# Front-projected DeltaNet columns stay raw until the mixers convolve them; decay matrices are made in other blocks, their rows loaded by SyncE

## The chip, the cores and the metric

The kernel runs on one NeuronCore of a Trainium2 chip. The metric is the device time of one execution in microseconds. Five engines run side by side, each from its own in-order queue: TensorE (PE, matmuls), VectorE (DVE), ScalarE (ACT), GpSimd (POOL) and SyncE (SP, which only starts transfers). They wait for each other through semaphores. A transfer can be started from the queue of SP, ACT or POOL.

## The reference

One decoder layer on 512 tokens of width 2048, all in float32. Cut to what matters here:

```
u    = rmsnorm(x, norm_w)
proj = u @ w_in                      # 2048 x 20528: q/k/v/o/z of 8 mLSTM heads,
                                     # q/k/v/z of 16 DeltaNet heads, gates, merge gates
# mLSTM branch: chunkwise, with exp(b_t - b_s + i_s) as decay matrix per head
# DeltaNet branch, 16 heads of 128:
qkv  = silu(causal_conv4(dn_qkv, dn_conv_w))       # 4 taps along the tokens, per channel
q, k = l2norm(q), l2norm(k)
gam  = cumsum(g)                                   # g <= 0, per head
D[t,s] = exp(gam[t] - gam[s]) for s <= t, else 0   # decay matrix per head
A    = strict_lower(beta * (k k^T) * D);  solve (I + A) w = rhs;  then chunk by chunk
h_b  = rmsnorm(o, dn_norm_w) * silu(dn_z)
out  = rmsnorm(x + sigmoid(ga) * (h_a @ w_out[:2048]) + sigmoid(gb) * (h_b @ w_out[2048:]))
```

## The kernel before

**Precision and bounds of the work.** Each float32 operand of a large matmul is split into a high and a low part (`split_hi` at L147 on ACT, `split_lo` at L150 on DVE), and each product is three matmuls (high by high, low by high, high by low). The activations are split once (`uh`, `ul`); the weights come in as raw tiles by SP and are split just ahead of their use.

**Stages, in PE's order.**
1. The front: seven projections of 256 DeltaNet columns each straight from the activations (`FRONT`, L170): the pair of k columns of heads 0 and 1, and v columns of six odd heads with those of other heads beside them, eight columns of 128 in all that are needed later (`PRE`). `spill` (L391) writes them raw, scaled by the token factor, to `raw_d` in DRAM.
2. The first stage: 14 blocks of `SEVEN`, each a Strassen-like 1024 x 1024 piece of the projection (`seven`, L617). A block has an A half of 8 quads with four products each, and a B half of 8 quads with three. A product is six 128 x 512 matmuls (L643 to L645), and after each one `tick()` lets the side tasks go on by one step. So a block has 56 ticks, 336 matmuls, and its A half ends at tick 32. The blocks are, in order: four for mLSTM z and o ("z"), two for DeltaNet z ("s"), one for mLSTM q and k ("q"), two for v, one "q", four for the merge gates ("g"). I call them blocks 0 to 13.
3. The mixers: eight units (`dn_unit`, L1304), unit p holding the DeltaNet heads 2p and 2p+1. In each, PE projects k, v and q columns while side tasks run the convolution, norms, triangular solve and recurrence of the heads; eight `ml_head` tasks run beside them.
4. The output projection: three plain blocks, two of the Strassen kind and a last one.

**The crossing.** In a block the PSUM results of the A half must be added up before the B half goes on in the same banks. ACT copies two of them (`copy1`, L628), and DVE does three pairs of additions through `add` (L700): m1 into `U1`, then U1 + m5 into `C22`, then m7 onto `C22`. B's matmuls on m5 wait for the second pair, those on m7 for the third. I call this place the crossing.

**Side tasks.** A task is a generator; its `yield n` asks to be resumed n ticks later, and `start` puts it on the list. PE's order is written by hand. On the other engines a scheduler orders the instructions by priority and its own estimate of when they are ready; `urgent` and `high_priority` raise some, and `behind("V")` (or "A", "S") makes an instruction come after the newest weight split of DVE (cast of ACT, weight load of SP). Weight splits and `add` have a raised priority. The table `ahead` (L940) says which side task starts in which block, at quad 5 of its A half (tick 20), but in the last block at its first quad:

- blocks 0 to 4: five `decay(n)` each (four in the last), one after the other. A decay matrix is made in a 128 x 512 tile: POOL loads the row of `gam` to all partitions (L885), 3 ticks later POOL masks it (`affine_select`, L892), 2 ticks later ACT takes the exponentials, all in one step (four activations at L902, or for odd DeltaNet heads, which are mirrored, twelve at L898 to L900), and ACT's queue stores it to `dm_d`.
- blocks 5 to 12: `scaled_u(2i)` and then `convolved(i)`. `scaled_u` (L853) makes the scaled activations of two of the sixteen 128-rows for a later stage: per row DVE adds (L863), multiplies (L866) and subtracts (L871), ACT casts (L868), two stores. `convolved` (L907) loads one raw column tile from `raw_d`, does the four taps (one ACT multiplication at L915, three DVE instructions at L918), silu on ACT (L922) and a 32 x 32 block transposition on DVE (L925), and stores the transposed tile to `pre_d` in 4 transfers with pieces of 128 bytes from ACT's queue (and, for the k columns, the plain tile to `kc_d`).
- block 13: `scaled_back`, which reads the scaled activations into `uh` and `ul`.

Those tasks and the block ends (`sink_...`) share four tiles of 128 x 512 (tag "wr", `spare` at L703).

**A unit of the mixers.** `conv_in` (L1010) copies a projected column tile from PSUM into one of two padded tiles `yp`; `conv_silu` (L1017) does the taps (ACT L1021, three DVE instructions L1023); `silu_end` (L1026) does silu (ACT L1028) and calls `turn` (L1041), which transposes 32 x 32 blocks on DVE (L1044) and sends the tile through DRAM, 4 writes of 128-byte pieces (L1060) and a read (L1063), all from SP. `dn_front_k` (L1066) forms k k^T (PE L1086), scales it, writes the diagonal blocks to DRAM and solves them on DVE in 31 steps of two small instructions (L1135, L1137); the result goes through DRAM (`xd`, L1149, and `tt`, L1150, from SP) and is transposed on DVE into `tn` (L1153). `dn_back` (L1178) starts with matmuls on `tn` (PE L1191). For the eight columns made ahead, `turned` (L1299) loads the finished tile from `pre_d`; unit 0 takes k from `kc_d`, and for units 1 to 6 (`VPRE`) the v columns of the odd head are the ones made ahead, so their v projection has one head only (`proj_half`).

## Time and profile before

| | us |
|---|---|
| median of 3 runs | 2180.43 |
| lowest, highest | 2177.93, 2183.38 |
| the profiled execution's own time | 2176.61 |
| its span, first to last instruction | 2174.4 |
| PE busy in it | 2124.8 (98%) |
| DVE busy | 1747.1 (80%) |
| ACT busy | 1102.4 (51%) |
| POOL busy | 503.1 (23%) |
| blocks 0 to 13 of the first stage | 116 to 1226 |
| mixers | 1226 to about 1860 |

How to read it: PE has work nearly all the time, and its instructions are fixed, so the time moves only where PE waits or where its clock is lowered. The waits of PE, and what ended each, are therefore read first, then PE's busy time in short stretches around the places where it waits, then what the engine that it waited for did there. The other engines' busy shares matter only where PE waits for them. In the block table of the page a PE share of 9 means 90% or more and hides waits of 2 us, so stretches of one block (76 to 81 us) or less are used. Starts of the A halves of blocks 0 to 13 are at 116, 200, 278, 358, 436, 512, 591, 670, 749, 830, 909, 988, 1068 and 1147 us, and of the B halves at 167, 247, 325, 405, 481, 558, 637, 715, 794, 875, 953, 1033, 1114 and 1192 us, read from the first matmuls on `su` and `s4` tiles.

### The profile page before, as it was taken

How to read it: one execution, taken by the hardware profiler on the slowest of the kernel's cores; microseconds unless marked ns; L12 is line 12 of the kernel's file. 1: busy time of each engine (PE TensorE's matmuls, PEld its weight loads, DVE VectorE, ACT ScalarE, POOL GpSimd, SP SyncE). 2: the span in 40 equal slices, each digit the busy share in tenths (PEclk: the TensorE clock that was granted, in tenths of full speed). 3: DMA queues.
4: the chain of work that ended last, by engine and by line, in shares of the span. 5: the costliest groups of instructions: out<-in, count | busy, mean ns of one | idle time of the engine just before them, and what ended most of it. 6: DMA issues, size and time to landing. Idle time of an engine off the chain costs nothing.

```text
span 2174.4 us, 32578 instructions
## 1 busy us (share of the span) xinstructions
PE 2124.8 (98%) x10507; PEld 1748.0 (80%) x10507; DVE 1747.1 (80%) x3022; ACT 1102.4 (51%) x2135; POOL 503.1 (23%) x745
## 2 busy tenths in 40 slices
PE   9999999999999999999999999999999999999998
PEld 7777778888778778787778888887888888887786
DVE  5978888798898888888788586796787789569787
ACT  4445665655554545444444444543644555345345
POOL 1231121010004000220000123434434444233221
PEclk9999999999999999999999999999999999999999
DMA  5466776777778867787769877877777868778796
GB/s 175 146 200 214 241 237 222 248 234 230 235 249 245 272 210 238 234 256 240 248 212 329 301 191 180 204 176 198 210 199 204 206 166 233 203 216 288 229 294 237
DMA packets 473828, 491.74 MB, mean 226 GB/s; under 512 B 192485, under 2 KB 304842, under 8 KB 473530
## 3 DMA queue, kind: packets, MB, share of 16 engines
q1 hardware_dynamic: 375898, 357.67, 55.5%
q0 software_dynamic: 28416, 83.65, 12.3%
q10 hardware_dynamic: 69344, 48.36, 6.9%
q8 instruction: 82, 1.34, 0.3%
q14 instruction: 88, 0.72, 0.1%
HBM read 376.71 MB, written 117.02 MB: 227 GB/s over the span
## 4 chain that ended last, share of the span: by engine, by line
PE 47%; DVE 4%; DMA 3%; issue 1%; ACT 1%; SPq 0%; DVEq 0%; POOLq 0%; POOL 0%; ACTq 0%
PE pj L292 11%; PE pj L290 6%; PE ps L644 5%; PE ps L643 5%; PE ps L645 5%; PE py L1580 2%; PE py L1582 2%; PE py L1581 2%; DMA wr<-in_w_out_dram 2%; PE pj L274 1%; PE pj L273 1%; PE pj L272 1%; DVE wl L150 1%; PE pk L1086 1%; PE pqk L1161 1%
## 5 line engine op out<-in xcount | busy, mean ns | idle before, releaser
L147 ACT CAST wh<-wr 128x512 fp32r<-128x512 f32 (+1 forms) x506 | 368.2, 729 | 374.4 <-PE pj L292 157.0
L150 DVE TENSOR_TENSOR wl<-wr,wh 128x512 fp32r<-128x512 f32 (+1 forms) x506 | 426.5, 844 | 157.3 <-ACT wh L147 145.2
L643 PE MATMUL ps<-wh,uh 128*128 128x512 f32 x800 | 314.4, 393 | 18.6 <-DVE X L700 18.6
L644 PE MATMUL ps<-wl,uh 128*128 128x512 f32 x800 | 313.5, 392 | 3.3 <-DVE wl L150 3.2
L645 PE MATMUL ps<-wh,ul 128*128 128x512 f32 x800 | 312.9, 391 | 0.0
L290 PE MATMUL pj<-uh,wh 128*128 128x512 f32 x672 | 284.7, 424 | 1.3 <-ACT qk L406 1.3
L147 ACT CAST wh<-t 128x1024 fp32r<-128x1024 f32 x128 | 135.0, 1055 | 293.9 <-PE ps L645 114.2
L292 PE MATMUL pj<-uh,wl 128*128 128x512 f32 x672 | 264.8, 394 | 0.6 <-DVE wl L150 0.6
L644 PE MATMUL ps<-wl,suh 128*128 128x512 f32 x672 | 262.2, 390 | 1.9 <-DVE wl L150 1.8
L292 PE MATMUL pj<-ul,wh 128*128 128x512 f32 x672 | 264.1, 393 | 0.0
L643 PE MATMUL ps<-wh,suh 128*128 128x512 f32 x672 | 262.0, 390 | 2.1 <-ACT wh L147 2.1
L645 PE MATMUL ps<-wh,sul 128*128 128x512 f32 x672 | 261.8, 390 | 0.0
L147 ACT CAST wh<-ts 128x512 fp32r<-128x512 f32 x256 | 158.2, 618 | 163.9 <-DVE ts L603 129.4
L598 POOL DMA_DIRECT2D t_d<-ts x112 | 61.7, 551 | 736.7 <-DVE ts L585 671.4
L150 DVE TENSOR_TENSOR wl<-t,wh 128x1024 fp32r<-128x1024 f32 x128 | 158.2, 1236 | 75.4 <-ACT wh L147 75.2
L150 DVE TENSOR_TENSOR wl<-ts,wh 128x512 fp32r<-128x512 f32 x256 | 176.1, 689 | 37.1 <-ACT wh L147 35.2
L643 PEld LDWEIGHTS ps<-wh,uh 128*128 128x128 f32 x800 | 150.7, 188 | 56.5 <-DVE X L700 25.1
L644 PEld LDWEIGHTS ps<-wl,uh 128*128 128x128 f32 x800 | 151.0, 189 | 36.5 <-DVE wl L150 5.7
L645 PEld LDWEIGHTS ps<-wh,ul 128*128 128x128 f32 x800 | 151.0, 189 | 31.5
L584 DVE TENSOR_TENSOR t<-wr 128x1024 f32<-128x1024 f32 x128 | 157.0, 1227 | 15.7 <-DMA wr<-in_w_in_dram 8.7
L644 PEld LDWEIGHTS ps<-wl,suh 128*128 128x128 f32 x672 | 126.2, 188 | 29.9 <-DVE wl L150 3.9
L643 PEld LDWEIGHTS ps<-wh,suh 128*128 128x128 f32 x672 | 126.1, 188 | 29.7 <-ACT wh L147 3.4
(372 smaller groups left out, 4141.6 us busy)
## 6 DMA issues: line engine op xcount, KB each, us to landing
wr<-in_w_in_dram SPq DMA_DIRECT2D x728, 256.0 KB, 4.0
wr<-in_w_out_dram SPq DMA_DIRECT2D x138, 256.0 KB, 5.0
t_d<-ts POOLq DMA_DIRECT2D x112, 256.0 KB, 4.3
wr<-t_d SPq DMA_DIRECT2D x112, 256.0 KB, 4.4
wr<-in_w_in_dram SPq DMA_DIRECT2D x48, 128.0 KB, 2.3
to<-rows_d POOLq DMA_DIRECT2D x24, 256.0 KB, 5.3
dm_d<-to ACTq DMA_DIRECT2D x24, 256.0 KB, 3.2
us_d<-uhi ACTq DMA_DIRECT2D x16, 256.0 KB, 3.6
```

Of the source, the lines that this page charges most:

```text
L147: newest["A"] = A.copy(hi, src).ins
L150: newest["V"] = V.tensor_tensor(out=lo, in0=src, in1=hi.bitcast(F32), op=ALU.subtract).ins
L290: T.matmul(ps[j], hi[:, k, wsl], uh[:, kt, :], start=(kt == 0), stop=False)
L292: T.matmul(ps[j], w[:, k, wsl], x_[:, kt, :], start=False, stop=(kt == KT - 1 and w is lo))
L584: V.tensor_tensor(out=t13, in0=r[:, 1:3, :], in1=r[:, 0:2, :], op=ALU.subtract)
L598: queue.dma_start(t2_d[b % 2, i], ts[:, 0, :])
L643: T.matmul(ps[t], ah, hi, start=(g == "A" and i == 0), stop=False, skip_group_check=True)
L644: T.matmul(ps[t], ah, lo, start=False, stop=False, skip_group_check=True)
L645: T.matmul(ps[t], al, hi, start=False, stop=(i == KH - 1), skip_group_check=True)
L1580: T.matmul(ps[c], uh[:, kt, tsl], hi, start=(kt == ks[0]), stop=False)
L1581: T.matmul(ps[c], uh[:, kt, tsl], lo, start=False, stop=False)
L1582: T.matmul(ps[c], ul[:, kt, tsl], hi, start=False, stop=(kt == ks[-1]))
```

## The change

- `convolved` is gone, with `pre_d` and `kc_d`. The eight column tiles stay raw in `raw_d`. In the mixers `conv_loaded` (new) loads one from `raw_d` into a `yp` tile by SP, 4 ticks later does the taps, 4 or 6 ticks later silu and `turn`, which is what the unit's own columns go through. For units 1 to 6 it starts 2 ticks after the k projection, ahead of the v projection; `dn_front_k` of unit 0 starts 6 ticks later than before, and its `dn_back` 5 ticks later.
- `scaled_u` moves from blocks 5 to 12 to blocks 1 to 8 and starts at quad 7 of the A half (tick 28) where it was quad 5.
- `decay` moves from blocks 0 to 4 to blocks 0, 9, 10, 11 and 12. The row is loaded by SP behind the newest weight load, not by POOL; the mask comes 5 ticks after it, not 3. The exponentials of the four chunks are 1 tick apart each, not in one step. The five decays of a block are started 6 ticks apart, so that they can overlap. The positive column for mirrored heads is copied once by DVE in `gates`, not made by POOL for each head.

```
-        G.dma_start(flat, rows_d[row, :].partition_broadcast(P))
-        if mirror:
-            pgam = sbp.tile([P, NC], F32, tag="pgam", name="pgam", bufs=1)
-            G.tensor_scalar(out=pgam, in0=bias, scalar1=-1.0, scalar2=None, op0=ALU.mult)
-        yield 3
+        with behind("S"):
+            nc.sync.dma_start(flat, rows_d[row, :].partition_broadcast(P))
+        yield 5
...
-        with behind("A"):
-            for c in range(NC):
+        for c in range(NC):
+            with behind("A"):
                 if mirror:
...
+            if c < NC - 1:
+                yield 1
+        with behind("A"):
             nc.scalar.dma_start(dm_d[n], flat)
         yield 1
-    def convolved(i):
...
-    ND = 5
-    ahead = [in_turn([decay(n) for n in range(ND * b, min(ND * b + ND, DNH + MLH))]) for b in range(ND)]
-    ahead += [in_turn([scaled_u(2 * i), convolved(i)]) for i in range(KH)]
-    ahead += [None] * (len(SEVEN) - len(ahead))
+    def decays(b):
+        for n in range(ND * b, min(ND * b + ND, DNH + MLH)):
+            start(decay(n))
+            yield 6
+
+    SLOTS = [0, *range(KH + 1, len(SEVEN) - 1)]
+    ND = -(-(DNH + MLH) // len(SLOTS))
+    ahead = [None] + [scaled_u(k) for k in range(0, KT, 2)] + [None] * (len(SEVEN) - KH - 1)
+
+    for i, b in enumerate(SLOTS):
+        ahead[b] = decays(i)
...
-                if b < len(beside) and beside[b] and n == (KH - 3 if b + 1 < len(beside) else 0):
+                if b < len(beside) and beside[b] and n == (0 if b + 1 == len(beside) else KH - 1 if 0 < b <= KH else KH - 3):
...
-    def turned(dst, i):
+    def conv_loaded(i, ct, dst, to, more=0):
+        yp = yps[cnt["yp"] % NYP]
+        cnt["yp"] += 1
         with behind("S"):
-            nc.sync.dma_start(dst, pre_d[i].rearrange("(n j) r a c -> (j r) n (a c)", n=NC))
-        yield 1
+            nc.sync.dma_start(yp[:, 3:S + 3], raw_d[i])
+        yield 4
+        conv_silu(None, ct, dst, yp=yp)
+        yield 4 + 2 * more
+        yield from silu_end(dst, (to if i > 1 else dst, to))
...
-                nc.sync.dma_start(kq[j][:, 0, :], kc_d[j])
-                start(turned(ke, j), 3 + j, front)
-        start(dn_front_k(hs, kq, u), 1, front)
+                start(conv_loaded(j, 16 + hs[j], kq[j][:, 0, :], ke, j), 1 + j, front)
+        start(dn_front_k(hs, kq, u), 1 if p else 7, front)
+        if p in VPRE:
+            vt = u["pool"].tile([P, NC, P], F32, tag="vn", name="vt", bufs=2)
+            start(conv_loaded(VPRE[p], 32 + hs[1], vt.rearrange("p c t -> p (c t)"), vt), 2, front)
+            u["vs"].append(vt)
...
-        start(dn_back(hs, kq, u), 28 - (p == 0) + last, by)
+        start(dn_back(hs, kq, u), 28 + 4 * (p == 0) + last, by)
```

PE's instructions stand in the same order up to the first matmul of unit 0's k k^T; after it, those of unit 0's tasks come some ticks later between the same projections, and over the last third of the program the order is the same again. The scheduled engines are reordered. In rows of the change the line numbers are those of the changed file: the weight split L150 is L148 there, L603 is L604, `add` L700 is L701, L863 is L864, L1149 and L1150 are L1124 and L1125, L1060 and L1063 are L1035 and L1038.

DVE at the crossing of block 5 (the additions are `X<-X,ps`, the chores of `scaled_u` write `ulo`), before:

```order
L150 TENSOR_TENSOR wl<-wr_5141,wh 128x1024
L603 TENSOR_TENSOR ts<-wr_5188 128x512
L863 TENSOR_TENSOR ulo<-uh,ul 128x512
L871 TENSOR_TENSOR ulo<-ulo,uhi 128x512
L700 TENSOR_TENSOR X<-X,ps 128x512 x2
L866 TENSOR_TENSOR ulo<-ulo,rr_5151 128x512
L150 TENSOR_TENSOR wl<-ts,wh 128x512
L700 TENSOR_TENSOR X<-X,ps 128x512 x2
L150 TENSOR_TENSOR wl<-wr_5188,wh 128x1024
L603 TENSOR_TENSOR ts<-wr_5233 128x512
L871 TENSOR_TENSOR ulo<-ulo,uhi 128x512
L700 TENSOR_TENSOR X<-X,ps 128x512 x2
```

and the same place in the change:

```order
L148 TENSOR_TENSOR wl<-wr_4941,wh 128x1024
L604 TENSOR_TENSOR ts<-wr_4986 128x512
L701 TENSOR_TENSOR X<-X,ps 128x512 x3
L148 TENSOR_TENSOR wl<-ts,wh 128x512
L701 TENSOR_TENSOR X<-X,ps 128x512 x3
L148 TENSOR_TENSOR wl<-wr_4986,wh 128x1024
L604 TENSOR_TENSOR ts<-wr_5024 128x512
L864 TENSOR_TENSOR ulo<-uh,ul 128x512
```

The first chore now stands behind all six additions, and so do the wide weight split and the subtraction for the quad after it. Before, blocks 5, 6, 8, 9, 11 and 12 had the order shown first, blocks 7 and 10 one much like it, blocks 0 and 2 a wide split and a subtraction ahead of the last addition but no chore, and blocks 1, 3, 4 and 13 the order shown second. In the change all blocks have the second order but blocks 9 and 11, which have that of blocks 0 and 2.

SP in the third unit of the mixers, between the k projection and the read of the solved blocks (`tt`), before:

```order
L1060 DMA td<-ke 32x16x32 x4
L195 DMA wr<-in_w_in_dram 128x2x256
L1149 DMA xd<-xi 256x1x32 x2
L1063 DMA ke<-td 128x4x128
L1149 DMA xd<-xi 256x1x32
L195 DMA wr<-in_w_in_dram 128x2x256
L1060 DMA td<-ke 32x16x32 x4
L1149 DMA xd<-xi 256x1x32
L1301 DMA vt<-pre_d 128x4x128
L1063 DMA ke<-td 128x4x128
L195 DMA wr<-in_w_in_dram 128x2x256
L1150 DMA tt<-xd 128x8x32
```

and in the change, from the new load of the raw tile on:

```order
L1278 DMA yp_11062<-raw_d 128x512
L193 DMA wr<-in_w_in_dram 128x2x256
L1035 DMA td<-ke 32x16x32 x4
L193 DMA wr<-in_w_in_dram 128x2x256
L1038 DMA ke<-td 128x4x128
L193 DMA wr<-in_w_in_dram 128x2x256
L1124 DMA xd<-xi 256x1x32
L1035 DMA td<-ke 32x16x32 x4
L1124 DMA xd<-xi 256x1x32 x2
L1038 DMA ke<-td 128x4x128
L193 DMA wr<-in_w_in_dram 128x2x256
L1124 DMA xd<-xi 256x1x32
```

The load of the raw tile stands ahead of the k tiles' trip, where the load of the finished tile stood behind it, and one of the four `xd` writes stands ahead of the second trip where two had. The `tt` read follows two loads of `g_d` later, and behind it come eight `td` writes for two v tiles where four stood before.

More of the change, by code (lines that the diff above doesn't have):

```diff
@@ L96, in hybrid_body @@
     raw_d = dr.tile([len(PRE), P, S], F32, tag="rawd", name="raw_d")
-    pre_d = dr.tile([len(PRE), 16, BS, 4, BS], F32, tag="pred", name="pre_d")
-    kc_d = dr.tile([2, P, S], F32, tag="kcd", name="kc_d")
     ident = cp.tile([P, P], F32, tag="ident", name="ident")
@@ L453, in hybrid_body @@
     beta = cp.tile([P, NC, DNH], F32, tag="beta", name="beta")
+    pgam = sbp.tile([P, NC, DNH], F32, tag="pgam", name="pgam")
     def gates():
@@ L539, in gates @@
         A.activation(negeg, pc[:, :, 16:32], AF.Exp)
+        V.tensor_copy(pgam, pc[:, :, 16:32])
         V.tensor_scalar(out=ngam, in0=pc[:, :, 16:32], scalar1=-1.0, scalar2=None, op0=ALU.mult)
@@ L899, in decay @@
                     A.activation(t[64:P, c, 64:P], t[64:P, c, 64:P], AF.Exp, bias=bias[64:P, c:c + 1])
-                    A.activation(t[64:P, c, 0:64], t[64:P, c, 0:64], AF.Exp, scale=-1.0, bias=pgam[64:P, c:c + 1])
+                    A.activation(t[64:P, c, 0:64], t[64:P, c, 0:64], AF.Exp, scale=-1.0, bias=pgam[64:P, c, n:n + 1])
                 else:
                     A.activation(t[:, c, :], t[:, c, :], AF.Exp, bias=bias[:, c:c + 1])
+            if c < NC - 1:
+                yield 1
@@ L903, in decay @@
+        with behind("A"):
             nc.scalar.dma_start(dm_d[n], flat)
         yield 1
-    def convolved(i):
-        raw = wp.tile([P, S], F32, tag="wr", name="pr0", bufs=NRAW)
-        with behind("S"):
-            nc.sync.dma_start(raw, raw_d[i])
-        yield 4
-        ct = PRE[i]
-        y = wp.tile([P, S], F32, tag="wr", name="py0", bufs=NRAW)
-        with behind("A"):
-            A.mul(y, raw, convc[:, 144 + ct:145 + ct])
-        for j in (2, 1, 0):
-            with behind("V"):
-                V.scalar_tensor_tensor(out=y[:, 3 - j:S], in0=raw[:, 0:S - 3 + j], scalar=convc[:, 48 * j + ct:48 * j + ct + 1],
-                                       in1=y[:, 3 - j:S], op0=ALU.mult, op1=ALU.add)
-            yield 1
-        with behind("A"):
-            A.activation(y, y, AF.Silu)
-        yield 1
-        with behind("V"):
-            V.transpose(raw, y)
-        if i < 2:
-            with behind("A"):
-                nc.scalar.dma_start(kc_d[i], y)
-        yield 2
-        ov = raw.rearrange("p (m c) -> p m c", c=BS)
-        for a in range(4):
-            with behind("A"):
-                nc.scalar.dma_start(pre_d[i, :, :, a, :].rearrange("m r c -> r m c"), ov[a * BS:(a + 1) * BS])
-            yield 1
@@ L936, in in_turn @@
-    def in_turn(jobs):
-        for job in jobs:
-            yield from job
-    ND = 5
-    ahead = [in_turn([decay(n) for n in range(ND * b, min(ND * b + ND, DNH + MLH))]) for b in range(ND)]
-    ahead += [in_turn([scaled_u(2 * i), convolved(i)]) for i in range(KH)]
-    ahead += [None] * (len(SEVEN) - len(ahead))
+    def decays(b):
[3 more added lines that the diff above has]
+    SLOTS = [0, *range(KH + 1, len(SEVEN) - 1)]
@@ L1318, in dn_unit @@
             else:
-                nc.sync.dma_start(kq[j][:, 0, :], kc_d[j])
-                start(turned(ke, j), 3 + j, front)
-        start(dn_front_k(hs, kq, u), 1, front)
+                start(conv_loaded(j, 16 + hs[j], kq[j][:, 0, :], ke, j), 1 + j, front)
[4 more added lines that the diff above has]
+            u["vs"].append(vt)
         ps = proj_half(DN_V + dcol) if p in VPRE else proj_cm(DN_V + dcol, evens=p == UNITS[0])
-        for j in range(2):
+        for j in range(len(ps)):
             vt = u["pool"].tile([P, NC, P], F32, tag="vn", name="vt", bufs=2)
-            u["vs"].append(vt)
-            if j < len(ps):
-                conv_silu(ps[j], 32 + hs[j], vt.rearrange("p c t -> p (c t)"))
-                start(silu_end(vt.rearrange("p c t -> p (c t)"), (vt, vt)), 4 + 3 * j, front)
-            else:
-                start(turned(vt, VPRE[p]), 6, front)
+            u["vs"].insert(j, vt)
+            conv_silu(ps[j], 32 + hs[j], vt.rearrange("p c t -> p (c t)"))
+            start(silu_end(vt.rearrange("p c t -> p (c t)"), (vt, vt)), 4 + 3 * j, front)
         if last:
```

1 line of the change is left out of this document (removed).

## The prediction

> **What bounds the kernel now.** First the head of the page, then the view of what PE waited for (columns: total us, times, longest us).
>
> ```profile
> span 2174.4 us, 32578 instructions
> ...
> PE ps L643 <- DVE X L700: 21.2, 20, 1.9
> PE ps L644 <- DVE wl L150: 5.7, 8, 1.6
> PE p L1191 <- DVE tn L1153: 2.9, 1, 2.9
> ...
> PE ps L643 <- ACT wh L147: 2.1, 3, 1.0
> ```
>
> PE waits little, and most of it for the additions of the crossing; the other rows are tens of times shorter. The program's PE order hardly moves, so I price stretches of the first stage by their length. The view of busy time in chosen stretches (columns: stretch, length, then busy us and instructions of PE, weight loads, DVE, ACT and POOL, granted clock, DMA share, GB/s) gives blocks 1, 2, 3, block 4, and blocks 5 to 12 together:
>
> ```profile
> 200.00:278.00 78.00, 76.78 (x338) 63.01 (x337) 63.95 (x81) 50.47 (x98) 15.78 (x24) 1.00 0.72 232
> 278.00:358.00 80.00, 77.72 (x336) 62.07 (x335) 66.19 (x84) 50.66 (x91) 14.69 (x22) 1.00 0.74 231
> 358.00:436.00 78.00, 76.87 (x338) 63.09 (x337) 65.61 (x83) 46.78 (x84) 12.00 (x19) 1.00 0.73 241
> 436.00:512.00 76.00, 76.00 (x337) 62.92 (x336) 65.00 (x83) 43.13 (x72) 9.77 (x16) 1.00 0.73 235
> 512.00:1147.00 635.00, 617.16 (x2689) 505.36 (x2688) 541.55 (x705) 316.35 (x451) 76.46 (x128) 0.99 0.76 239
> ```
>
> Block 4 has PE busy for all of its 76.0 us, so 76 us is a block without a wait. Blocks 1 to 3 together are 236 − 3 × 76 = 8.0 us longer, blocks 5 to 12 are 635 − 8 × 76 = 27.0 us longer. That is the stock from which the change can gain.
>
> The same view around crossings: of block 4, of block 5, then the sum of eight such 12 us stretches (blocks 5 to 12), and the sum of two (blocks 0 and 2).
>
> ```profile
> 477.00:489.00 12.00, 12.00 (x55) 9.93 (x54) 10.63 (x16) 6.57 (x12) 0.00 (x0) 1.00 0.75 238
> ```
>
> ```profile
> 554.00:566.00 12.00, 9.71 (x42) 7.41 (x41) 10.79 (x17) 4.33 (x7) 0.00 (x0) 1.00 0.87 264
> ```
>
> ```profile
> sum 96.00, PE 79.72 PEld 61.10 DVE 93.56 ACT 38.53 POOL 0.00; mean PE 9.97 PEld 7.64 DVE 11.70 ACT 4.82 POOL 0.00
> ```
>
> ```profile
> sum 24.00, PE 19.66 PEld 13.69 DVE 18.27 ACT 15.37 POOL 1.75; mean PE 9.83 PEld 6.85 DVE 9.13 ACT 7.69 POOL 0.88
> ```
>
> In blocks 5 to 12 DVE is busy for 93.56 of 96 us while PE stands for 16.3 of them (96 − 79.72). In blocks 0 and 2 PE stands for 4.3 us of 24, 2.2 each, with DVE busy for only three quarters. So there are two kinds of late addition: one behind too much DVE work, one behind work that itself waits. The timeline of DVE at block 5's crossing (start, us, operation) shows the first kind:
>
> ```profile
> 553.95 0.69 DVE L871 TENSOR_TENSOR ulo<-ulo,uhi 128x512 fp32r<-128x512 f32 x1
> 554.55 1.28 DVE L700 TENSOR_TENSOR X<-X,ps 128x512 f32<-128x512 f32 x2
> 555.75 0.69 DVE L866 TENSOR_TENSOR ulo<-ulo,rr 128x512 f32<-128x512 f32 x1
> ...
> 556.95 1.28 DVE L700 TENSOR_TENSOR X<-X,ps 128x512 f32<-128x512 f32 x2
> 558.14 1.22 DVE L150 TENSOR_TENSOR wl<-wr,wh 128x1024 fp32r<-128x1024 f32 x1
> 559.28 0.68 DVE L603 TENSOR_TENSOR ts<-wr 128x512 f32<-128x512 f32 x1
> 559.88 0.69 DVE L871 TENSOR_TENSOR ulo<-ulo,uhi 128x512 fp32r<-128x512 f32 x1
> 560.48 1.28 DVE L700 TENSOR_TENSOR X<-X,ps 128x512 f32<-128x512 f32 x2
> ```
>
> The last pair, for which B's matmuls on m7 wait, starts 5.9 us after the first (560.48 − 554.55), behind two chores of `scaled_u` (L866 and the second L871), a wide split and a subtraction. In block 4 the second three additions start 2.4 us after the first three:
>
> ```profile
> 477.19 1.88 DVE L700 TENSOR_TENSOR X<-X,ps 128x512 f32<-128x512 f32 x3
> ...
> 479.58 1.87 DVE L700 TENSOR_TENSOR X<-X,ps 128x512 f32<-128x512 f32 x3
> ```
>
> **The crossings.** In the change the order of every block but 9 and 11 is the one that block 4 has, with the chores behind the additions. I therefore take the whole excess of blocks 5 to 12 away, −27.0, and give back two crossings of the kind of blocks 0 and 2 for blocks 9 and 11. Such a crossing costs its 2.2 us of idle and some refilling: the eight crossings' 16.3 us of idle belong to 27.0 − 3.4 (the clock, below) = 23.6 us of excess, though part of that is waits elsewhere in the block, so I take 2.7 each, +5.4. Block 0's crossing loses its lateness too, −2.7. Bounds: the order decides nothing, 0; no crossing late, −29.7.
>
> **The clock inside these 27 us.** Twice among blocks 5 to 12 the granted clock fell right after a crossing; a third time in the mixers:
>
> ```profile
> 795.00:805.00 10.00, 8.12 (x28) 6.20 (x28) 6.45 (x10) 3.36 (x5) 0.00 (x0) 0.83 0.73 240
> 1034.00:1044.00 10.00, 8.12 (x29) 6.18 (x28) 6.45 (x10) 3.44 (x5) 0.00 (x0) 0.83 0.72 237
> 1468.00:1482.00 14.00, 11.14 (x112) 8.65 (x110) 6.98 (x24) 6.34 (x20) 8.13 (x11) 0.76 0.79 186
> ```
>
> 0.17 of 10 us is 1.7 us each, 3.4 us for the first two. PE's idle in those stretches is under 2 us (10 − 8.12), and the longest wait for X is 1.9 us, so the fall followed a short wait here; without the wait I expect no fall. *A rule against this:* the Trainium skill, page "TensorE: Matmul & The Clock Gate", section "HAM oscillation — how this bites in real kernels", gives idle gaps over about 3.4 us as what lowers the clock. By it the falls would not be due to these waits; the rows show shorter ones ahead of each, so the measurement goes against the figure. I keep "the falls stay" as a rival, priced from the rows.
>
> **Blocks 1 to 3.** Block 2 loses a crossing like block 0's. Blocks 1 and 3 have no late crossing; what they wait for is a lump of twelve exponentials of a mirrored decay in ACT's queue ahead of a cast (first, last, and the cast behind them):
>
> ```profile
> 234.30 0.40 ACT L898 ACTIVATE to<-to,ngam 64x128 f32<-64x128 f32 x1
> ...
> 238.01 0.33 ACT L900 ACTIVATE to<-to,pgam 64x64 f32<-64x64 f32 x1
> 238.36 0.62 ACT L147 CAST wh<-ts 128x512 fp32r<-128x512 f32 x1
> ```
>
> 4.1 us of ACT stand ahead of that cast. The decays leave these blocks, so I take all 8.0 us away. Bounds: 0 to −8.0.
>
> **What the moved tasks cost where they go.** `scaled_u` brings six DVE and two ACT instructions to the B half of blocks 1 to 8: 6 × 0.69 = 4.1 us of DVE (the rows of L866 and L871), over some ten ticks of 76 / 56 = 1.36 us. The B quads are three ticks, 4.1 us, long, and carry a wide split, a subtraction and a narrow split: 1.22 + 0.68 + 0.69 = 2.6 us. Each quad thus has 1.5 us of DVE free, and 4.1 us fit into three of them. Nothing but a chance collision is left: 0.25 us a block, +2. If that cover were gone, 4.1 us a block. The decays in blocks 9 to 12 bring ACT the same exponentials in four portions of about 1.0 us (4.1 / 4) with a tick between; ACT is busy for 4.82 of 12 us at the crossings, so a portion fits in. The row loads leave POOL's queue for SP's:
>
> ```profile
> to<-rows_d POOLq DMA_DIRECT2D x24, 256.0 KB, 5.3
> ```
>
> 5.3 us to landing against the 5 ticks (6.8 us) that the mask now comes later. On SP weight loads stand behind each, and a row load that must wait for one of the four shared tiles holds them. I take 0.5 us for each of these four blocks, +2 (bounds 0 and 5.3 each). What leaves blocks 5 to 12 besides is `convolved`, with its share of the end-of-block waits for wl (L644 in the first fence); that is inside the 27.0.
>
> **The mixers.** Eight columns are now convolved there. Rows of the view of groups from 1226 us to the end of the mixers (columns: count, then total us and mean ns):
>
> ```profile
> L1023 DVE SCALAR_TENSOR_TENSOR kq<-yp,convc,kq 128x512 f32<-128x512 f32 x90 | 65.8, 741 | 3.4 <-ACT kq L1021 3.2
> L1021 ACT ACTIVATE kq<-yp,convc 128x512 f32<-128x512 f32 x30 | 22.0, 732 | 0.9 <-PE po L1255 0.4
> L1044 DVE STREAM_TRANSPOSE to<-vt 128x512 f32<-128x512 f32 x10 | 7.0, 702 | 2.6 <-DMA h_d<-to 2.5
> ```
>
> One costs DVE 3 × 0.74 + 0.70 = 2.9 us, eight 23.4 us. Seven of them begin in units 0 to 6 right after the k projection. The seven 20 us stretches after it, and all of the units:
>
> ```profile
> sum 140.00, PE 139.94 PEld 117.97 DVE 115.25 ACT 97.80 POOL 56.75; mean PE 19.99 PEld 16.85 DVE 16.46 ACT 13.97 POOL 8.11
> ```
>
> ```profile
> sum 609.00, PE 604.43 PEld 506.05 DVE 477.72 ACT 307.54 POOL 238.58; mean PE 75.55 PEld 63.26 DVE 59.72 ACT 38.44 POOL 29.82
> ```
>
> Over whole units DVE goes from 478 to 501 of 609 us, and the 40 convolutions already there leave PE only 4.6 us idle: that speaks for nearly 0. But right after k, DVE's 16.46 of 20 us becomes 19.4, and low parts of weights stand in the same queue. Bounds 0 and 23.4 us; nearer to 0 by the idle, so I take a quarter, +6. In it is the third unit's wait for `tn`. The view of that tile:
>
> ```profile
> L1191 PE MATMUL p<-tn,aq x256: 191/191/254, 1315.8 to 1860.0; 32*32 32x32 f32 x128
> ...
> L1153 DVE STREAM_TRANSPOSE tn<-tt x8: 426/438/445, 1308.3 to 1854.7; 128x256 f32<-128x256 f32 x8
> ```
>
> The first `tn` is done 7.1 us ahead of its matmul (1315.8 − 1308.3 − 0.44), the last at most 4.9 (1860.0 − 1854.7 − 0.44), and only the third is late, by 2.9. A piece of a trip takes 3.2 us to landing:
>
> ```profile
> td<-ke SPq DMA_DIRECT2D x56, 64.0 KB, 3.2
> ```
>
> In front of the `tt` read SP now has two more loads and a changed order of trips.
>
> **The sum**, on the profiled execution's own 2176.61 us (2.2 more than its span): −8.0 − 27.0 + 5.4 − 2.7 = −32.3 for the crossings and the lumps, +2 +2 for the moved tasks, +6 for the mixers: −22.3, so 2154.3. That execution is 3.8 us under the median of 2180.43, against which the change is compared, so the forecast is **2158 us**.
>
> **The rivals.**
> - *The falls of the clock stay*, for they need not come from these waits: 3.4 us of the gain is missing, 2161.5. For it: only two of eight late crossings have one. Against: each stands right behind a wait.
> - *The waits move into the B halves.* DVE is busy for 541.55 of 635 us in blocks 5 to 12, and what doesn't fall at the crossing falls elsewhere; chores ahead of a narrow split make `wl` late (the 5.7 us of the second waits row show that it happens). Half of 32.3 is kept: 2176.6 − 16.2 + 6 + 3.8 = 2170. Against: 1.5 us free in each quad.
> - *The mixers pay in full*, 23.4 where I have 6: 2175.5. For: 19.4 of 20 us. Against: 78% over the units, and the raised priority of splits.
> - *Row loads hold SP* in blocks 9 to 12: 4 × 5.3 = 21.2 where I have 2: 2177.3. Against: weight loads run ahead of their splits, since no wait of PE for a transfer stands among the rows of the first fence.
> - *Slower: the trip of the solved blocks gets late in the units.* SP is in order, and the new load, eight transfers for v and a second trip for k in unit 0 stand among the `xd` writes and around `tt`. Where `tn` is late PE waits as in the third unit: in the third clock row 14 − 11.14 = 2.9 us idle and 0.24 × 14 = 3.4 us of clock, 6.3 us a unit. From 2154.3 on, the fourth further unit (22.3 / 6.3 = 3.5) makes it slower; with six further, units 0 to 6, 2154.3 + 37.8 + 3.8 = 2196. Against: up to 7.1 and 4.9 us in hand in the first and last unit, two and one and a half transfers of 3.2 us.
>
> **How the numbers follow.** The forecast has 0.55, the clock 0.08, the B halves 0.15, the mixers in full 0.10, the row loads 0.05, the late trips 0.07. The forecast's own range is 2148 to 2168. With everything at its best (no give-back, no allowance, the third unit's wait gone too: −37.7 − 6.3) it is 2136; 2146 leaves out about 0.03 there. Up to 2174 the range takes in the clock, the B halves and four tenths of the mixers' case, and leaves out the rest, some 0.17. About 0.3%, 6.5 us, is what can be told from no change here: faster means below 2173.9. Faster 0.55 + 0.08 + 0.15 + 0.04 = 0.82; same 0.06 + 0.05 = 0.11; slower 0.07.
>
> **What would show it.** Right: no wait of PE on the additions but in blocks 9 and 11 (under 6 us in all), blocks 1 to 8 at 76 to 77 us, the granted clock at 1.00 up to 1200 us, and units with under 12 us of idle. Wrong: waits for `wl` in the B halves of blocks 1 to 8; PE idle behind SP in blocks 9 to 12; new waits at L1191 in several units, each with a lowered clock behind it.

## The result and the profile after

The change makes the kernel faster: 2165.65 us median (2165.52 to 2169.89, 4 runs) against 2180.34 (2177.93 to 2183.38), a ratio of 0.9937 with a 95% interval of 0.9919 to 0.9954. That is 14.7 us where 22 were forecast, inside the range. The profiled execution took 2165.53 us, with a span of 2163.8.

What the forecast was made of went two ways. First, busy time in stretches (columns as before) for blocks 1 to 4 and 5 to 12, in the changed kernel:

```profile
193.00:269.00 76.00, 76.00 (x337) 62.94 (x336) 67.07 (x89) 39.15 (x56) 4.13 (x8) 1.00 0.70 228
269.00:345.00 76.00, 76.00 (x337) 62.94 (x336) 67.12 (x89) 39.08 (x57) 4.32 (x8) 1.00 0.75 225
345.00:421.00 76.00, 76.00 (x337) 62.90 (x337) 67.07 (x89) 39.08 (x57) 4.32 (x8) 1.00 0.67 225
421.00:497.00 76.00, 76.00 (x337) 62.91 (x336) 67.11 (x89) 39.62 (x57) 4.32 (x8) 1.00 0.69 221
497.00:1113.00 616.00, 611.64 (x2689) 503.57 (x2688) 510.06 (x649) 338.28 (x550) 97.48 (x153) 1.00 0.76 247
```

Blocks 1 to 4 take 76.0 us each with PE busy throughout, though DVE has more to do in them than before. Blocks 5 to 12 take 616 us where they took 635, at a granted clock of 1.00. What is left above 76 us a block stands in blocks 9 and 11:

```profile
802.00:882.00 80.00, 77.81 (x340) 63.14 (x339) 60.70 (x75) 47.20 (x91) 10.65 (x17) 1.00 0.70 238
882.00:958.00 76.00, 75.99 (x336) 62.60 (x334) 65.34 (x83) 48.97 (x91) 31.22 (x47) 1.00 0.86 267
958.00:1037.00 79.00, 76.84 (x335) 62.38 (x334) 59.45 (x74) 44.27 (x78) 10.12 (x14) 1.00 0.75 251
1037.00:1113.00 76.00, 76.00 (x337) 62.91 (x336) 59.77 (x75) 40.97 (x68) 7.26 (x12) 1.00 0.75 251
```

PE's instructions number the same in both programs, so the start of the n-th one can be compared. At the end of the first stage the profiled execution of the change is 34.0 us ahead of that of the kernel before. At the end of the program it is 10.9 us ahead: the mixers and what follows took 23.1 us back. PE's waits in the changed kernel:

```profile
PE ps L644 <- DVE X L701: 4.9, 6, 1.3
PE pr L1225 <- DVE st L1244: 4.1, 3, 2.9
PE p L1166 <- DVE tn L1128: 4.0, 1, 4.0
PE pnum L1368 <- DVE c L1378: 3.1, 1, 3.1
...
PE p L1166 <- DVE cs L1072: 2.2, 1, 2.2
PE pk L1061 <- ACT vt L996: 2.1, 1, 2.1
```

The additions fell from 21.2 us to 4.9, of which 4.2 lie in blocks 9 and 11. All the other rows shown are in the mixers, and five of these waits lie in stretches with a lowered clock (the granted clock stands third from the end of a row):

```profile
1240.00:1255.00 15.00, 11.91 (x46) 9.40 (x45) 12.58 (x40) 4.71 (x12) 1.98 (x2) 0.89 0.42 109
1295.00:1305.00 10.00, 7.85 (x86) 5.86 (x87) 4.40 (x8) 6.39 (x20) 7.68 (x10) 0.66 0.76 177
1450.00:1460.00 10.00, 7.12 (x90) 5.68 (x93) 5.92 (x23) 3.72 (x11) 6.05 (x10) 0.66 0.80 154
1558.00:1570.00 12.00, 9.07 (x36) 7.67 (x36) 9.72 (x28) 2.32 (x5) 3.09 (x6) 0.72 0.89 257
1683.00:1690.00 7.00, 4.89 (x19) 3.87 (x18) 6.73 (x19) 3.99 (x12) 0.78 (x2) 0.76 0.93 219
sum 54.00, PE 40.83 PEld 32.49 DVE 39.35 ACT 21.13 POOL 19.58; mean PE 8.17 PEld 6.50 DVE 7.87 ACT 4.23 POOL 3.92
```

In these 54 us PE stands for 13.2 (54 − 40.83), and the lowered clock costs 0.11 × 15 + 0.34 × 10 + 0.34 × 10 + 0.28 × 12 + 0.24 × 7 = 13.5. The kernel before lost 2.9 and 3.4 us in the one such stretch it had there. The difference, 20.4 us, is most of the 23.1.

What stands ahead of the late `c` and `st` was found in DVE's row of waits, of the kernel before and of the change:

```profile
DVE tmp L1135 <- DMA ls<-ld: 3.6, 1, 3.6
```

```profile
DVE tmp L1110 <- DMA ls<-ld: 20.2, 6, 7.3
```

The front did not name these tiles. In `dn_front_k` the diagonal blocks of A go to DRAM in eight small writes from SP (`ld`), come back in four reads (`ls`), and after `yield 9` the 31 solve steps begin on DVE with `tmp<-ls,xi`. The first step has a fixed place in DVE's queue. If `ls` has not landed, DVE stands, and everything queued behind it with it. The timeline of DVE in the change shows it, in unit 0, where PE waits 3.1 us for `c`, in unit 4, where it waits 2.9 us for `st`, and in unit 2, where it waits 0.9 us for `st`:

```profile
1242.00 0.19 DVE L1110 TENSOR_TENSOR tmp<-ls,xi 128x31 f32<-128x31 f32 x1 [7.32 <-DMA ls<-ld]
...
1248.05 0.48 DVE L1378 SCALAR_TENSOR_TENSOR c<-c,de,pcs 128x257 f32<-128x257 f32 x1
```

```profile
1556.52 0.19 DVE L1110 TENSOR_TENSOR tmp<-ls,xi 128x31 f32<-128x31 f32 x1 [5.50 <-DMA ls<-ld]
...
1560.69 0.28 DVE L1244 COPY st<-pst 128x128 f32<-128x128 f32 x1
```

```profile
1400.83 0.19 DVE L1110 TENSOR_TENSOR tmp<-ls,xi 128x31 f32<-128x31 f32 x1 [3.46 <-DMA ls<-ld]
1400.93 0.75 DVE L998 SCALAR_TENSOR_TENSOR kq<-yp,convc,kq 128x512 f32<-128x512 f32 x1
1401.59 0.28 DVE L1244 COPY st<-pst 128x128 f32<-128x128 f32 x1
```

DVE has been idle for 7.32, 5.50 and 3.46 us, and `c` or `st`, for which PE waits, comes out behind the step and the splits and taps that had piled up. SP's timeline tells why `ls` was late; the kernel before first, then the change, both unit 2:

```profile
1401.04 0.38 SPq L1063 DMA_DIRECT2D vt<-td  x1
...
1402.06 3.74 SPq L1113 DMA_DIRECT2D ld<-aq  x8
...
1406.97 1.71 SPq L1124 DMA_DIRECT2D ls<-ld  x4
```

```profile
1381.83 0.81 SPq L1088 DMA_DIRECT2D ld<-aq  x2
1384.25 1.93 SPq L1035 DMA_DIRECT2D td<-to  x4
...
1386.76 0.47 SPq L1088 DMA_DIRECT2D ld<-aq  x1
1387.33 3.09 SPq L1035 DMA_DIRECT2D td<-to  x4
...
1392.61 1.94 SPq L1088 DMA_DIRECT2D ld<-aq  x4
...
1396.68 1.73 SPq L1099 DMA_DIRECT2D ls<-ld  x4
```

From the first `ld` to the first `ls` it was 4.9 us (1406.97 − 1402.06), and is 14.9 (1396.68 − 1381.83): the trips of two v tiles stand between the eight writes. Only units 0 and 2 have the row of writes torn apart like this (in unit 0 it was 7.1 us and is 10.4). In unit 4 the row is as short as before, 6.5 us, but eight `td` writes (5.3 us of SP) stand just ahead of it where four (2.8 us) did. I had not read this when I planned the first experiments; it came out of their failures.

### The profile page after: what moved, and what is told of

Read it like the earlier page. It is cut to its first block, busy times and chain, and to the rows that moved or that the text cites. A ratio compares the mean times of both kernels' runs of the same rounds, so it can differ in the third digit from the quotient of the medians.

```text
span 2163.8 us, 32569 instructions
## 1 busy us (share of the span) xinstructions
PE 2122.6 (98%) x10507; PEld 1751.5 (81%) x10507; DVE 1745.2 (81%) x3023; ACT 1097.7 (51%) x2135; POOL 483.8 (22%) x713
## 4 chain that ended last, share of the span: by engine, by line
PE 77%; DVE 9%; DMA 5%; issue 2%; ACT 2%; SPq 1%; POOL 0%; DVEq 0%; ACTq 0%; POOLq 0%
PE ps L645 18%; PE ps L644 18%; PE ps L646 18%; PE pj L290 7%; PE pj L288 4%; PE py L1560 2%; PE py L1561 2%; PE py L1562 2%; DVE wl L148 2%; DVE tmp L1110 1%; DVE xi L1112 1%; DVE kq L998 1%; DMA h_d<-to 1%; DMA yp<-raw_d 1%; DMA wr<-in_w_in_dram 0%
## 5 line engine op out<-in xcount | busy, mean ns | idle before, releaser
L148 DVE TENSOR_TENSOR wl<-wr,wh 128x512 fp32r<-128x512 f32 (+1 forms) x506 | 427.4, 846 | 151.1 <-ACT wh L145 135.9
L148 DVE TENSOR_TENSOR wl<-t,wh 128x1024 fp32r<-128x1024 f32 x128 | 156.7, 1224 | 78.7 <-ACT wh L145 78.6
L148 DVE TENSOR_TENSOR wl<-ts,wh 128x512 fp32r<-128x512 f32 x256 | 176.0, 688 | 26.2 <-ACT wh L145 24.5
L290 PEld LDWEIGHTS pj<-uh,wl 128*128 128x128 f32 x672 | 128.3, 191 | 28.4 <-DVE wl L148 1.0
L288 PEld LDWEIGHTS pj<-uh,wh 128*128 128x128 f32 x672 | 129.1, 192 | 25.0 <-ACT qk L404 1.7
```

The source lines that it names most:

```text
L148: newest["V"] = V.tensor_tensor(out=lo, in0=src, in1=hi.bitcast(F32), op=ALU.subtract).ins
L288: T.matmul(ps[j], hi[:, k, wsl], uh[:, kt, :], start=(kt == 0), stop=False)
L290: T.matmul(ps[j], w[:, k, wsl], x_[:, kt, :], start=False, stop=(kt == KT - 1 and w is lo))
```

## The experiments

Runs on different chips had the kernel before at 2180 to 2185 us, so ratios to it are compared. "Lead" is the profiled execution's lead over that of the kernel before at the end of the first stage and at the end of the program, in us, and the last column is DVE's waits for `ls`.

| run | median | ratio (95%) | lead | `ls` |
|---|---|---|---|---|
| the change | 2165.65 | 0.9937 (0.9919–0.9954) | 34.0, 10.9 | 20.2 |
| start at quad 7 alone | 2161.49 | 0.9923 (0.9899–0.9947) | 19.5, 16.2 | 8.5 |
| convolutions ahead, B half | 2157.68 | 0.9900 (0.9878–0.9923) | 28.5, 23.1 | 4.6 |
| mixers' part alone | 2203.07 | 1.0111 (1.0088–1.0134) | −5.4, −32.1 | 25.2 |
| later v | 2178.26 | 0.9988 (0.9973–1.0003) | 34.1, −2.4 | 37.6 |
| no taps | 2166.34 | 0.9919 (0.9891–0.9946) | 33.8, 6.1 | 29.3 |
| no trips | 2173.20 | 0.9949 (0.9930–0.9967) | 33.7, 3.7 | 23.8 |
| k columns ahead | 2158.39 | 0.9884 (0.9852–0.9915) | 31.8, 19.7 | 13.0 |
| convolutions ahead, A half | 2154.85 | 0.9868 (0.9840–0.9896) | 29.0, 26.2 | 6.4 |
| the same, unit 0 late | 2160.81 | 0.9893 (0.9866–0.9920) | 29.5, 23.9 | 19.2 |
| the change, `ld` first | 2151.68 | 0.9856 (0.9836–0.9877) | 33.4, 23.0 | 4.1 |
| convolutions ahead, A half, `ld` first | 2145.29 | 0.9841 (0.9819–0.9863) | 33.0, 32.0 | none |

**The crossing by itself.** One condition in the kernel before:

```
-    n == (KH - 3 if b + 1 < len(beside) else 0)
+    n == (0 if b + 1 == len(beside) else KH - 1 if b >= 5 else KH - 3)
```

> The kernel before with one edit: the tasks of blocks 5 to 12 (scaled activations, then the convolution made ahead) start at quad 7 of the A half, not quad 5. Theory (the crossing's additions were late only because the first chores stood ahead of them on VectorE): the waits for X at the eight crossings go, 16.3 us of idle and 3.4 us of clock with them; the convolutions then run in the B halves and cost up to 3 us in late weight splits. 2155 to 2161. Rival (the gain of the first stage came from taking the convolutions and their 128-byte writes out, and the moment of the start matters little): the waits stay or move into the B halves, within 6 us of before.

A ratio of 0.9923, just above the range that the theory gave. PE's order is the same, and 635 us of blocks 5 to 12 became 616:

```profile
511.00:1127.00 616.00, 612.54 (x2690) 503.61 (x2689) 540.09 (x705) 317.14 (x449) 76.48 (x128) 1.00 0.77 246
```

So the first chores' place ahead of the additions was the cause, as forecast, and DVE does its 540 us there as before. The convolutions in the B halves leave waits of 0.5 to 1.1 us at the block ends. The units and what follows lose 3.3 us; the largest new wait there is one for `st` of 3.6 us with its lowered clock.

**The two halves of the change, each without the other.** First the change with `convolved`, `turned` and `dn_unit` of the kernel before:

```
-    ahead = [None] + [scaled_u(k) for k in range(0, KT, 2)] + ...
+    ahead = [None] + [in_turn([scaled_u(2 * i), convolved(i)]) for i in range(KH)] + ...
```

> The changed kernel with the mixers of before: the eight columns are convolved ahead again, each behind the scaled activations of its block (blocks 1 to 8, start at quad 7). Theory (the first stage gained 34 us and the mixers gave 23 back, apart from each other): 23 us under the changed kernel, less up to 4 us for the convolutions in the B halves: 2142 to 2147. Rival (the convolutions in the first stage cost there what they now cost in the mixers): 2158 to 2168.

The first stage keeps 28.5 of 34.0 us, and the mixers lose 5.4. The median of 2157.68 is at the edge of what the rival gave, the profiled execution 2153.2; between the two expectations. Faster than the change, in any case: the convolutions cost less in the first stage (34.0 − 28.5 = 5.5 us) than in the mixers (23.1 − 5.4 = 17.7 us). Then the other half, the mixers' part put into the kernel before:

```
-    ahead += [in_turn([scaled_u(2 * i), convolved(i)]) for i in range(KH)]
+    ahead += [scaled_u(2 * i) for i in range(KH)]
...  (conv_loaded and dn_unit as in the change)
```

> The kernel before, with the eight convolutions taken from the first stage to the mixers as in the change, and nothing else: scaled activations in blocks 5 to 12 from quad 5, decays in blocks 0 to 4 in a lump, rows by GpSimd. Theory: the crossings stay late (about 16 us idle), the end-of-block waits of blocks 7 and 10 go (2 us), the mixers lose 20 to 25 us: 2195 to 2203. Rival (the convolutions were what made the first stage late): the first stage gains 15 us or more and the whole stays under 2186.

2203 us, as the theory had it. The first stage gains nothing from being rid of the convolutions; its waits on the additions stay:

```profile
PE ps L641 <- DVE X L698: 21.6, 20, 1.9
```

It even loses 5.4 us, 3.4 of it since the clock fell after four crossings of blocks 5 to 12 here where it fell after two before. The mixers lose 26.7. So the gain of the first stage comes without the mixers' part, and the loss of the mixers without the first stage's. The two halves do not add up, though: their leads at the end, 23.1 and −32.1 us, make −9.0, and the change has 10.9.

**Place or sum of work in the mixers.** In the change, for units 1 to 6:

```
-            start(conv_loaded(VPRE[p], 32 + hs[1], ..., vt), 2, front)
+            start(conv_loaded(VPRE[p], 32 + hs[1], ..., vt), 8, front)
```

> The changed kernel; in units 1 to 6 the raw v tile is loaded 8 ticks after the k projection, not 2, so that its taps and its trip come behind the trip of the previous unit's solved blocks. If the mixers lose by place (a few late hand-overs in SP's and VectorE's queues just behind k): the waits in the third, fourth and seventh unit (4.0, 2.9 and 2.1 us, each with about 2 to 3.4 us of clock) go, those of unit 0 (3.1 and 2.2) stay: 10 to 16 us faster than the change, 2150 to 2156. If they lose by the sum of VectorE's work: within 3 us of the change.

Both expectations missed: it is slower by 12.6 us in the median. My theory had been that the load crowds SP's queue just behind k. Later, it does more harm: DVE waits for `ls` in seven units, and PE for `st` in four.

```profile
DVE tmp L1110 <- DMA ls<-ld: 37.6, 7, 8.0
```

```profile
PE pr L1225 <- DVE st L1244: 12.0, 4, 3.6
```

**DVE's work or SP's trips.** Two kernels that leave out part of the eight columns' treatment in the mixers, first the taps, then the trip:

```
-        conv_silu(None, ct, dst, yp=yp)
+        with urgent(1):
+            A.mul(dst, yp[:, 3:S + 3], convc[:, 144 + ct:145 + ct])
```

> The changed kernel; the eight columns convolved in the mixers keep their load, their multiplication on ScalarE, silu, transposition and trip, but the three tap instructions on VectorE (2.2 of 2.9 us each) are left out, so these columns hold other values. If VectorE's work in that place is what makes hand-overs late: half or more of the 23 us that the mixers lost come back, 2145 to 2154. If SP's additional transfers are: within 4 us of the change, 2162 to 2169.

```
-        yield from silu_end(dst, (to if i > 1 else dst, to))
+        with behind("A"):
+            A.activation(dst, dst, AF.Silu)
+        ...   (transposition only)
```

> The changed kernel; the eight columns are loaded, convolved and transposed in blocks in the mixers, but their trip through DRAM (four writes and a read on SP) is left out, so these tiles hold other values. If SP's additional transfers make the hand-overs of the solved blocks late: the waits for tn in units 0 and 2 (2.2 and 4.0 us) and their lowered clock go, 10 us or more, 2148 to 2156. If VectorE's work is the cause: within 4 us of the change, 2162 to 2169.

Neither gives the loss back. Without 18 us of taps (8 × 2.2) the ratio's interval covers the 0.9937 of the change, and the wait for `c` grew from 3.1 to 5.1 us; without the trips the change is no better either. So neither DVE's sum nor the number of SP's transfers makes the 23 us alone. What all of these have and the kernel before does not stood in DVE's waits: 29.3 and 23.8 us for `ls`. In the run without taps the first of them was 9.39 us long, and the late `c` came out behind it. In unit 2 of the run without trips the eight writes are still torn apart, 12.6 us from the first `ld` to the first `ls`, by the trip of the one v tile that is left. So one trip at that place is enough.

**Which columns.** In the change, the two k columns of unit 0 convolved ahead (blocks 1 and 2), unit 0 as in the kernel before; the six v columns stay in the mixers:

```
+                nc.sync.dma_start(kq[j][:, 0, :], kc_d[j])
+                start(turned(ke, j), 3 + j, front)
...
-        start(dn_front_k(hs, kq, u), 1 if p else 7, front)
+        start(dn_front_k(hs, kq, u), 1, front)
```

> The changed kernel; only the two k columns of unit 0 are convolved ahead again (in blocks 1 and 2, behind the scaled activations), unit 0 starts as before; the six v columns stay in the mixers. By the waits of the changed kernel unit 0 costs 5.2 us of idle and about 5 of clock of the 23: 2154 to 2158 if these go. If the loss is spread evenly over the eight columns: a quarter, 6 us, 2159 to 2161.

The two k columns are half of the loss: the mixers lose 12.1 us where they lost 23.1, and the ratio is 0.9884. The first expectation was right on the size. Whether it is their work or unit 0's later start, the next kernel but one asks.

**The convolutions in the A half.** As in the second run, but each convolution starts at quad 1, the scaled activations 24 ticks later (quad 7), the decays of blocks 9 to 12 at quad 6:

```
+    def both(i):
+        start(convolved(i))
+        yield 24
+        yield from scaled_u(2 * i)
```

> The changed kernel with the mixers of before (as in the run that put the convolutions back behind the scaled activations), but each convolution starts at quad 1 of the A half of its block, ahead of the crossing, where VectorE has 4 ticks a quad; and the decays of blocks 9 to 12 start at quad 6, so that no mirrored exponentials stand at the crossing. If the 5.5 us that the first stage lost there to the convolutions came from their place in the B half, they come back, and with the two late crossings of blocks 9 and 11 (5 us): 2145 to 2150. If the convolutions cost the same anywhere: 2151 to 2155.

A ratio of 0.9868. The two late crossings are gone, but in their stead PE waits for ACT at the ends of blocks 9 to 11 (2.0, 1.6 and 1.4 us), where the last decay's exponentials now stand ahead of the block end's own activations. With the median at 2154.85 and the profiled execution at 2150, this is nearer to "the same anywhere".

**Unit 0's later start alone.** In that kernel, with no convolution of these columns in the mixers at all:

```
-        start(dn_front_k(hs, kq, u), 1, front)
+        start(dn_front_k(hs, kq, u), 1 if p else 7, front)
...
-        start(dn_back(hs, kq, u), 28 - (p == 0) + last, by)
+        start(dn_back(hs, kq, u), 28 + 4 * (p == 0) + last, by)
```

> The kernel with all convolutions ahead at quad 1 (no convolution made ahead is left to the mixers), and as the only edit unit 0's two starts as in the change: its k task 6 ticks and its back task 5 ticks later. If half of the 23 us that the mixers lost comes from unit 0 being late against unit 1 (and not from the work of its two k columns): 8 to 12 us slower than without the edit, a ratio of 0.991 to 0.992 (0.9868 without). If it comes from their work: within 3 us of 0.9868.

The time doesn't settle it: 0.9893, between the two expectations, with an interval that covers both. The trace does on the mechanism: with nothing but those two starts moved, DVE's waits for `ls` went from 6.4 to 19.2 us, in six units and not in unit 0 alone.

```profile
DVE tmp L1151 <- DMA ls<-ld: 19.2, 6, 5.8
```

How much of the 11 us of the k columns that is stays open, for these waits don't turn into PE's in full: with 19.2 us of them the mixers lose 5.6 us here (2.8 without the edit), and 23.1 in the change with 20.2. So the sum of these waits does not by itself give the loss.

**The suspected cause alone.** The change, with its work as it is, and a raised priority for `ld` and `ls` on SP:

```
-                nc.sync.dma_start(ld[...], aq[bs, :, 0, bs])
+                with urgent(3):
+                    nc.sync.dma_start(ld[...], aq[bs, :, 0, bs])
...
-            nc.sync.dma_start(ls[...], ld.rearrange("g b s t -> (g b) s t"))
+            with urgent(3):
+                nc.sync.dma_start(ls[...], ld.rearrange("g b s t -> (g b) s t"))
```

> The changed kernel with one edit in the mixers: the eight writes of the diagonal blocks (ld) and the four reads of them (ls) have a raised priority on SP, so that they stand in a row and not among the v tiles' trips. Theory: the mixers lose because, with two v tiles on a trip, ls lands late, and VectorE's first solve step, whose place in its queue is fixed, holds everything behind it (waits of the solve step for ls: 3.6 us before, 20.2 in the change; 29.3 without the taps, 23.8 without the trips, 37.6 with the later load, 4.6 and 6.4 with the convolutions ahead). Then these waits fall under 8 us and 8 us or more come back: a ratio to the kernel before of 0.988 to 0.990 (0.9937 for the change). Rival: late ls is only a sign of a generally late unit; the wait moves to the taps, st or tn and the ratio stays at 0.992 to 0.995.

2151.68 us, a ratio of 0.9856 (0.9836 to 0.9877), clear of the change's. SP's timeline in unit 2, and DVE's waits:

```profile
1376.36 4.34 SPq L1089 DMA_DIRECT2D ld<-aq  x8
1380.80 0.91 SPq L1035 DMA_DIRECT2D td<-to  x2
1381.93 2.99 SPq L1101 DMA_DIRECT2D ls<-ld  x4
1384.97 3.14 SPq L1035 DMA_DIRECT2D td<-to  x6
```

```profile
DVE tmp L1112 <- DMA ls<-ld: 4.1, 3, 2.9
```

5.6 us from the first `ld` to the first `ls` where it was 14.9; the waits of DVE fell from 20.2 us to 4.1, and the mixers' loss from 23.1 to 10.4. The trips still run, behind. That is the cause shown by removing it: of the 23 us, 13 were the place of the eight small writes and the four reads in SP's queue. How much of the 13 came through DVE standing still and how much through solved blocks that were ready earlier is not separated. The rest is not settled. In this run it is three waits for `tb` (ACT) of 4.5 us in all and seven others between 0.4 and 1.7, with one lowered clock.

**A ladder of waits.** In the change, at each crossing but those of blocks 0, 9 and 11, DVE copied one PSUM tile onto itself 3 to 7 times ahead of the last addition:

```
+            if t:
+                for _ in range(EXTRA.get(b, 0)):
+                    with urgent(3):
+                        V.tensor_copy(m7, m7)
             add(c22, c22, m7)
```

> The changed kernel; at the crossings of blocks 1 to 8, 10, 12 and 13 VectorE copies one PSUM tile onto itself 3, 4, 5, 6, 7, 3, 4, 5, 6, 7 and 4 times (about 0.7 us each) ahead of the last addition, so that PE waits there for lengths between nothing and some 4 us. If the clock falls after each wait over 2 us and in none under 1.5 us: falls in the blocks with 5 copies and more. If a fall needs an idle gap over 3.4 us: in the blocks with 6 or 7 copies at most.

Inconclusive: PE's waits came to 5.4 to 10.2 us (2289 us in all), and the clock fell after every one. A copy took the 0.7 us that I had taken, and each further one made the wait 0.73 us longer, but with three copies it was already 7.2 us, for other work of DVE stood between the copies. It says nothing on waits of 1.5 to 3.5 us. The waits of all the other profiles do; they stand in the last section.

**Both together.** The convolutions in the A half from quad 2, decays 5 ticks apart, and `ld` first:

```
-        yield 24
+        yield 20
...
-            yield 6
+            yield 5
```

> The kernel with the convolutions ahead, from quad 2 of the A half of blocks 1 to 8 (quad 1 in the run before of this kind), the decays of blocks 9 to 12 from quad 6 and 5 ticks apart (6 before, where the last decay's exponentials stood ahead of the block's end and PE waited 2.0, 1.6 and 1.4 us there), and the raised priority of ld and ls on SP. By the traces: 29 us of the first stage in the run before of this kind, and 5 of those waits back, and its 2.8 us of loss in the mixers back: a ratio of 0.982 to 0.985, the fastest of all. If the waits at the block ends stay or come back elsewhere, and the convolutions in the first stage cost what the mixers now pay with ld first: 0.985 to 0.988, the same as the change with ld first.

2145.29 us, 0.9841: by the ratio 35 us under the kernel before, and clear of the change. Against the change with `ld` first the intervals overlap, so which of these two is better is not shown. The waits for `ls` are gone from DVE's list, and the mixers lose 1.0 us. Of the block ends' waits those of blocks 10 and 11 (0.7 and 1.2 us) are left, and one for a weight split of 1.65 us at 878 us.

## Why the prediction was right, and where its terms were not

**The crossings: right.** Blocks 5 to 12 lost their late additions but for blocks 9 and 11, which were named. The forecast was −27.0 + 5.4, with 4 us of allowances for the moved tasks. Measured were −19.0, with some 7 us left at the two late blocks (80 and 79 us where 76 is free of waits) and nothing for the moved tasks: blocks 1 to 4 at 76.0 us show that six more DVE instructions fit into a B half, and 76.0 in blocks 10 and 12 that SP's row loads held nobody. The start at quad 7 alone shows the order to be the cause, and the mixers' part alone that it was not the convolutions. One reading was wrong without harm: the other rows of PE's waits that the prediction shows (5.7, 2.9 and 2.1 us) are four to ten times shorter than the additions' 21.2 us, not tens of times.

**Blocks 1 to 3: right.** 8.0 us forecast, 8.0 measured (236 to 228).

**Block 0: mis-sized.** 2.7 forecast, 6.2 measured. Beside the crossing, the wait for a weight split at 130 us went from 1.35 to 0.85 us and the fall of the clock behind it (1.7 us) did not come. The prediction's rows left that fall out. In the eleven runs with the change's decays it did not come, and the wait there was 0.85 us at most; in the kernel before and the two with the old decays (the start at quad 7 alone, the mixers' part alone) it came, behind a wait of 1.35 to 1.37 us. What made that wait shorter is not shown.

**The clock: half right.** In the first stage no fall is left, as forecast from the rows. But the same reasoning, that a fall follows a short wait, had to be carried into the mixers: the five long waits there paid about twice. I priced the mixers' term without it, and used the pair of 2.9 and 3.4 us only in the slower rival.

**The mixers: the step that failed.** "I take a quarter, +6" was 23.1. The bounds of 0 and 23.4 held, and the rival "the mixers pay in full" had the size, but not its reason: without the taps the loss stays. I weighed DVE's sum of work, 16.46 of 20 us becoming 19.4, and SP's trip of the solved blocks. The link that broke is one step ahead of that trip in the same queue, the eight `ld` writes and the `ls` reads, whose lateness stops DVE at a fixed place. I had looked at SP's order only between k and `tt`, and read the row for `tn`, which is the longest wait of the mixers in PE's list before. The row of DVE for `ls`, 3.6 us in one unit, was in the trace of before: it said that this hand-over had no slack in that unit. The prediction's own sign, under 12 us of idle in the units, failed with it: PE stands for 18.6 us of the mixers' 660.

**The base: off by 3.7.** I added 3.8 us since the profiled execution of before lay under its median. That of the change lay 0.1 under its own. Stage by stage the traces differ by 11, the medians by 14.7; that offset is spread among runs and not a part of a forecast.

**The sum.** First stage −34.0 for −28.3, mixers +23.1 for +6: the profiled execution came out at 2165.5 for 2154.3. Two errors of opposite sign, 5.7 and 17.1. That the median lies inside the range is in part luck: had the first stage gained only the 28.3 us of the forecast, it would have been near 2171, above the 2168 of the range.

## What to carry to other kernels

When work moves into a stage, look not only at how full its engines are but at every instruction whose place in an in-order queue was chosen for a transfer that lands just in time: here the sum of DVE's work could be cut by 18 us without effect, while eight 16 KB writes and their reads, put in a row, were worth 14 us. Such a place can show ahead of the change as a small wait of an engine that is not the bottleneck, in that engine's own list of waits, as here in one unit of eight. And a chore that stands ahead of a hand-over need not go: started two quads later it stopped costing (19.5 us here), while taking other chores out of the same blocks brought nothing.

## What the runs showed of the hardware

The clock falls after waits shorter than I had thought needed, and not always. In 13 profiles (all but the ladder) between 140 and 2100 us, PE's waits by length, and how many had a lowered granted clock around them:

| wait, us | waits | with a lowered clock |
|---|---|---|
| 1.0 to 1.73 | 68 | 0 |
| 1.73 to 2.0 | 25 | 10 |
| 2.0 to 2.3 | 10 | 7 |
| 2.3 to 2.66 | 7 | 5 |
| over 2.66 | 21 | 21 |

Ahead of 140 us, which the table leaves out, three falls came behind waits of only 1.35 to 1.37 us (those of block 0 above). Equal waits can go either way: in the run with the convolutions ahead in the B half, two waits of 2.38 us, around the first the clock at 1.00, around the second at 0.79.

```profile
1441.00:1449.00 8.00, 5.62 (x54) 4.46 (x53) 5.93 (x19) 2.66 (x7) 2.72 (x6) 1.00 1.01 238
1626.00:1634.00 8.00, 5.74 (x24) 4.90 (x25) 7.88 (x22) 1.25 (x2) 1.78 (x3) 0.79 0.77 196
```

What decides between them can be read from the traces. Wherever a trace has more than one fall, they start whole steps of 3.413 us apart (in the change 14, 59, 91 and 128 steps after the first) and last one step or more at half clock. Cut all 14 profiles, the ladder's too, into such steps from about 105 to 2100 us (counted from a fall, or from the clock's first rise where there is none), and sort the steps at full clock by how long PE stands in them:

| PE idle in a step, us | steps | with a fall at their end |
|---|---|---|
| under 1.0 | 8028 | 0 |
| 1.0 to 1.70 | 76 | 3 (those of block 0) |
| 1.70 to 1.85 | 14 | 5 |
| 1.86 and more | 53 | 53 |

The first wait of 2.38 us lies across a border, with 1.82 us in one step and 0.56 in the next; the second has 2.34 us in one step.

A fall costs 0.21 × 8 = 1.7 us here, and 3.4 in other stretches. So a wait of 1.7 us is most often worth its length, one of 2.7 us about twice its length. The Trainium skill, page "TensorE: Matmul & The Clock Gate", section "HAM oscillation — how this bites in real kernels", gives gaps over about 3.4 us as the rule; 22 falls after waits of 1.73 to 2.66 us differ from it, and the measurement decides. The same page of the Trainium skill, in Part 1, says that the activity window is free-running; the traces agree, for the steps of 3.413 us keep their beat through a whole execution, wherever the waits fall.
